# A decoder of two layers in float32r: tile offsets, the first phase and retention's values

## The chip, the core and the metric

One core of one Trainium2 chip runs the whole program in one launch. The time is that of the device from start to end of an execution, in microseconds; beside it stands the span, from the first to the last instruction of one execution that the hardware profiler recorded.

## The reference

256 tokens of width 2048 go through two layers; the first mixes tokens by two kinds of attention, the second by retention. Behind each mixer stand cross-attention to 256 memory rows and a feed-forward part with a convolution over three tokens. All is float32.

```python
def reference(x, mem, positions, ...):
    mem_n = _rmsnorm(mem, norm_mem)
    h = x
    for l in range(DEPTH):
        hn = _rmsnorm(h, norm_mix[l])
        if l % 2 == 0:
            h = h + _mixer_ab(hn, ...)          # block and compressed/selected/window attention
        else:
            h = h + _mixer_c(hn, ...)           # retention
        h = h + _cross_attn(_rmsnorm(h, norm_cross[l]), mem_n, ...)
        h = h + _conv_ffn(_rmsnorm(h, norm_ffn[l]), ...)
    return _rmsnorm(h, norm_final)

def _retention(q, k, v):                        # 8 heads, dk 256, dv 512, chunks of 128
    def step(state, xs):
        qi, ki, vi = xs
        intra = einsum(einsum(qi, ki) * decay, vi)
        cross = einsum(qi, state) * q_dec
        state = state * c_dec + einsum(ki * k_dec, vi)
        return state, intra + cross
```

## The kernel before, in words

Nearly all time goes to products of activations with weights. [...] The weight products use fp32r and split each operand into an upper part (rounded to fp32r) and a lower part (the rest): upper x upper, upper x lower, lower x upper make three products. `weights` (L225) loads 128x1024 pieces of weights by SP's queue, ScalarE writes the upper part (L232), VectorE the lower one (L233).

Two forms of a product exist. `product_b_steps` has weights as the stationary operand and gives outputs with features on the partitions: the upper weights (L272) meet a moving slab of upper and lower tokens side by side, 512 columns, the lower weights (L277) its upper half, 256 columns. `product_a_steps` has tokens stationary and weights moving, 512 columns in most products, 256 and 280 in two early ones (L307 to L309). Each matmul has its own weight load.

Products follow each other without a gap in TensorE's order. Side tasks (attention heads, norms, retention's scores) are generators in a queue, `side`; `pump` (L244) lets the first two of them go a step at each turn of a product, and where a generator yields nothing it places its instructions there. TensorE's order is that of the code; in the first phase (L379 to L414) that of ScalarE and VectorE too; else a scheduler sets it.

The first phase multiplies x with 512 columns of weights before any norm factor is known: `x_in` holds x, `SPANS` (L365) groups its 16 slabs of 128 features in pairs, and each pair is loaded (`load_x`, L371, and L393), split (L197, L200, L401 to L407) and used in two products at once. Their results are added up by `halves` (L326 on ScalarE, L328 on VectorE), which frees the accumulators for the next product (L307). Meanwhile `start_steps` loads the rows of x and squares them on ScalarE (`Norm.add`, L148) for the norm.

In retention a head's scores `pr` (keys x tokens) and values `v` are plain fp32 and meet in three matmuls (L986, L988) that a side task, `attend`, places inside the next product, that of the gate.

Tiles come from a pool in which a tile takes its bytes per partition rounded up to 32. `eps`, one column of 4 bytes, is the first whose 32 bytes are no multiple of 64. As the built program has it, all large tiles that fp32r matmuls read begin 32 bytes behind a multiple of 64. Slabs inside tiles are whole multiples of 64 bytes apart, but for the weights of the 280-column product: three slabs of 1120 bytes stand side by side, so every third (30 of its 96 moving operands) begins on a multiple of 64.

Of the kernel before, what the change touches and what calls it, by code (L numbers as in the profile page):

```python
# [20 lines left out]
P = 128  # L21
# [54 lines left out]
def hybrid_kernel(ctx: ExitStack, tc: tile.TileContext, a, out):  # L76
# [6 lines left out]

    def new(shape, dt=F32, tag=None, bufs=1):
        count[0] += 1
        name = f"t{count[0]}"
        return sb.tile(shape, dt, name=name, tag=tag or name, bufs=bufs)

# [3 lines left out]
    def long():  # L92
        return new([P, 512], F32, "long", 9)
# [15 lines left out]


    ident = new([P, P])
    make_identity(nc, ident)
    ones = new([P, P])
    pool.memset(ones, 1.0)
    eps = new([P, 1])
# [4 lines left out]
    def raw_tile():  # L120
        return new([P, 1024], F32, "raw", 4)
# [242 lines left out]
    held = [[], []]  # L364
    SPANS = [range(k, k + 2) for k in range(0, ND, 2)]  # L365
    ready = [deque(), deque()]
# [3 lines left out]

    def load_x(p):  # L371

        nc.sync.dma_start(x_in[p].rearrange("p s t -> p (s t)"), a["x"][:, 2 * p * S : (2 * p + 2) * S])

# [4 lines left out]
    with tc.manual_schedule(engines=engines):  # L379
        act.activation(new([P, 1]), eps, AF.Copy, scale=eps)  # L380
        load_par(nc.sync, "mix")
        for p in range(ND // 2):
            i, c = p // 2, slice(p % 2 * 512, p % 2 * 512 + 512)
            if p % 2 == 0:
                raws = [raw_tile() for _ in range(2)]
                his = [new([P, 1024], F32R, "whi", 4) for _ in range(2)]
                los = [new([P, 1024], F32R, "wlo", 4) for _ in range(2)]
            if p < 4:
                load_x(p)
            for q in range(2):  # L390
                if p < 4 or p % 2 == 0:
                    d = c if p < 4 else slice(0, 1024)
                    nc.sync.dma_start(raws[q][:, d], w_ab.part(4 * i, 4, 4096 + 256 * q, 256)[:, d])  # L393
            if p == 3:
                for x in range(4, 8):
                    load_x(x)
            for s in (2 * p, 2 * p + 1):
                xs_mix.append(slab_tile())
                xhat_hi(xs_mix[s], x_in[p][:, s % 2, :], gain("mix")[:, s : s + 1])
            if p == 0:  # L400
                dve.tensor_copy(his[0][:, c], raws[0][:, c])  # L401
            for s in (2 * p, 2 * p + 1):
                xhat_lo(xs_mix[s], x_in[p][:, s % 2, :], gain("mix")[:, s : s + 1])
            for q in range(2):
                if p or q:
                    act.activation(his[q][:, c], raws[q][:, c], AF.Copy)
                dve.tensor_sub(los[q][:, c], raws[q][:, c], his[q][:, c].bitcast(F32))  # L407
# [3 lines left out]
            if p == 3:  # L411
# [205 lines left out]
    def mixer_ab(xs, row, col, kcv):  # L617
# [6 lines left out]
        def start_steps():  # L624
            norm = Norm()
            tg = [(t, g) for g in range(4) for t in range(2)]
            for i in range(10):
                if i < 8:
                    load_rows(*tg[i])
                if i > 1:  # L630
                    norm.add(*tg[i - 2])
                if i < 9:
                    yield
            norm.column(col)
            yield
# [6 lines left out]
            yield from angle_steps(0, posi)  # L642
# [19 lines left out]
        def compress(i, kind, t, done):  # L662

            for _ in range(8):
                yield
# [77 lines left out]
        comp = []  # L743
        side.extend((start_steps(), setup_steps()))
        side.append(compress(0, "k", kcv[0], comp))
# [22 lines left out]
        def nsa_group(g, qr, qu):  # L768
# [33 lines left out]
            side.extend(nsa_head(g, r, qr[r]) for r in range(4))  # L802
            yield
            yield
            yield
# [4 lines left out]
            dve.tensor_copy(pct, b[:, 0:S])  # L810
            pcts[g] = pct

        def nsa_head(g, r, q):
            h = 4 * g + r
            p_s = causal(q, ks[0][:, g, :], gate_v[:, :, h, 1])
            p_w = causal(q, ks[1][:, g, :], gate_v[:, :, h, 2])
            yield
            yield
            t_s = causal_t(p_s)
            yield  # L820
            t_w = causal_t(p_w)
            yield
            while len(comp) < 2:
# [104 lines left out]
    def mixer_c(xs, norm, done):  # L928
# [25 lines left out]
        def head(h, os):  # L954
# [16 lines left out]
            def attend():  # L971
# [241 lines left out]
```

## Time and profile before

| | us |
|---|---|
| median of 3 runs | 2832.78 (2832.66 to 2833.45) |
| the profiled execution | 2834.51 |
| its span | 2832.8 |
| TensorE matmul busy | 2812.4 |
| VectorE busy | 1906.3 |
| ScalarE busy | 1460.1 |

A row of a timeline gives start, duration, engine, line and operation, operands, count, and in brackets the idle time before it with what ended it. [...] A group's busy time is that of the union of its records.

### The profile page before, as it was taken

The page shows a single profiled execution, that of the slowest core. Times are in us where ns is not written, and L with a number is a line of the kernel's source. Part 1 is how long each engine was busy: PE and PEld are TensorE (multiplying, and loading weights), DVE is VectorE, ACT ScalarE, POOL GpSimd, SP SyncE. Part 2 cuts the span into 40 slices and gives each one's busy share as a digit, 9 for nine tenths or more (in the row PEclk, how much of TensorE's full clock was granted, in tenths as well). Part 3 has the DMA queues.
Part 4 walks back from the last instruction along what each step waited for, and adds up shares of the span by engine and source line. Part 5 has one row for each costly group of instructions (what it writes and reads, how often), then busy time and mean ns, then how long its engine had stood idle before and what let it go on. Part 6 is the DMA issues. An engine that isn't in the chain of part 4 may idle for free.

```text
span 2832.8 us, 39488 instructions
## 1 busy us (share of the span) xinstructions
PE 2812.4 (99%) x14726; PEld 2406.5 (85%) x14726; DVE 1906.3 (67%) x3147; ACT 1460.1 (52%) x2193; POOL 29.9 (1%) x211
## 2 busy tenths in 40 slices
PE   8999999999999999999999999999999999999998
PEld 7888888888888888888888888888888888888887
DVE  7765776776767677665555555556767767676766
ACT  6454455654545455454444444444665645454544
POOL 0000000000000000000000000000000000000000
PEclk9999999999999999999999999999999999999999
DMA  8535565455555555555555555555545555555554
GB/s 305 171 126 161 180 211 172 170 189 192 187 198 190 189 196 201 194 179 179 179 178 186 193 178 179 182 206 189 189 164 193 186 196 184 193 193 187 197 186 158
DMA packets 150544, 530.11 MB, mean 187 GB/s; under 512 B 17040, under 2 KB 17456, under 8 KB 150352
## 3 DMA queue, kind: packets, MB, share of 16 engines
q1 hardware_dynamic: 148752, 523.65, 54.7%
q0 software_dynamic: 1024, 2.90, 0.3%
q8 instruction: 115, 1.88, 0.3%
q10 hardware_dynamic: 576, 1.05, 0.1%
q14 instruction: 77, 0.63, 0.1%
HBM read 525.43 MB, written 2.10 MB: 186 GB/s over the span
## 4 chain that ended last, share of the span: by engine, by line
PE 98%; DMA 1%; ACT 0%; DVE 0%; SPq 0%; issue 0%; ACTq 0%; DVEq 0%
PE acc L272 32%; PE acc L277 17%; PE acc L307 14%; PE acc L309 14%; PE acc L308 14%; PE bank L350 1%; PE bank L986 0%; DMA t<-in_w_in_ab_dram 0%; PE bank L504 0%; PE bank L496 0%; PE bank L484 0%; DMA t<-in_rows_dram 0%; PE bank L1009 0%; PE bank L589 0%; PE bank L579 0%; PE bank L975 0%
## 5 line engine op out<-in xcount | busy, mean ns | idle before, releaser
L233 DVE TENSOR_TENSOR t<-t,t 128x1024 fp32r<-128x1024 f32 x954 | 1156.6, 1220 | 568.7 <-ACT t L232 522.9
L232 ACT ACTIVATE t<-t 128x1024 fp32r<-128x1024 f32 x954 | 1004.6, 1057 | 739.6 <-PE acc L309 540.6
L272 PE MATMUL acc<-t,t 128*128 128x512 f32 x4096 | 965.9, 391 | 6.2 <-DVE t L200 6.2
L272 PEld LDWEIGHTS acc<-t,t 128*128 128x128 f32 x4096 | 759.7, 188 | 159.1 <-DVE t L200 6.2
L307 PE MATMUL acc<-t,t 128*128 128x512 f32 (+2 forms) x1824 | 713.3, 391 | 4.9 <-DVE t L328 4.9
L309 PE MATMUL acc<-t,t 128*128 128x512 f32 (+2 forms) x1824 | 705.1, 387 | 0.0
L308 PE MATMUL acc<-t,t 128*128 128x512 f32 (+2 forms) x1824 | 704.5, 386 | 0.0
L277 PEld LDWEIGHTS acc<-t,t 128*128 128x128 f32 x4096 | 510.6, 192 | 11.6 <-issue 0.4
L277 PE MATMUL acc<-t,t 128*128 128x256 f32 x4096 | 518.0, 283 | 0.0
L307 PEld LDWEIGHTS acc<-t,t 128*128 128x128 f32 x1824 | 343.9, 189 | 74.7 <-DVE t L328 5.4
L309 PEld LDWEIGHTS acc<-t,t 128*128 128x128 f32 x1824 | 343.6, 188 | 69.5
L308 PEld LDWEIGHTS acc<-t,t 128*128 128x128 f32 x1824 | 343.9, 189 | 68.9 <-issue 1.9
L883 ACT ACTIVATE t<-acc 128x256 f32<-128x256 f32 x176 | 65.8, 374 | 229.6 <-PE acc L272 229.6
L886 DVE TENSOR_TENSOR t<-acc,t 128x256 f32<-128x256 f32 x176 | 74.1, 421 | 157.2 <-ACT t L883 157.2
L889 ACT ACTIVATE t<-t,t 128x256 f32<-128x256 f32 x176 | 103.8, 590 | 1.1
L210 ACT ACTIVATE t<-t 128x256 fp32r<-128x256 f32 x88 | 36.1, 411 | 130.5 <-DVE t L908 130.5
L607 DVE TENSOR_TENSOR t<-t,acc 128x512 f32<-128x512 f32 x148 | 95.1, 680 | 2.8 <-PE acc L1104 2.8
L891 DVE SCALAR_TENSOR_TENSOR t<-t,t,t 128x256 f32<-128x256 f32 x176 | 84.2, 478 | 1.5
L890 DVE SCALAR_TENSOR_TENSOR t<-t,t,t 128x256 f32<-128x256 f32 x176 | 84.2, 478 | 0.2
L326 ACT ACTIVATE t<-acc 128x256 f32<-128x256 f32 x80 | 30.0, 376 | 103.4 <-PE acc L272 103.4
L328 DVE TENSOR_TENSOR t<-acc,t 128x256 f32<-128x256 f32 x80 | 33.4, 419 | 69.7 <-ACT t L326 69.7
L887 DVE TENSOR_TENSOR t<-t,t 128x256 f32<-128x256 f32 x176 | 74.3, 422 | 3.0
(218 smaller groups left out, 1127.6 us busy)
## 6 DMA issues: line engine op xcount, KB each, us to landing
t<-in_w_up_dram SPq DMA_DIRECT2D x352, 512.0 KB, 3.4
t<-in_w_in_c_dram SPq DMA_DIRECT2D x192, 512.0 KB, 3.5
t<-in_w_down_dram SPq DMA_DIRECT2D x176, 512.0 KB, 3.4
t<-in_w_in_ab_dram SPq DMA_DIRECT2D x80, 512.0 KB, 4.2
t<-in_w_out_c_dram SPq DMA_DIRECT2D x64, 512.0 KB, 3.3
t<-in_w_out_ab_dram SPq DMA_DIRECT2D x32, 512.0 KB, 4.2
t<-in_w_kv_x_dram SPq DMA_DIRECT2D x32, 512.0 KB, 3.8
t<-in_w_q_x_dram SPq DMA_DIRECT2D x16, 512.0 KB, 3.2
```

Source lines behind the costliest of these rows:

```text
L232: act.activation(hi[:, 0 : m * ncol], raw[:, 0 : m * ncol], AF.Copy)
L233: dve.tensor_sub(lo[:, 0 : m * ncol], raw[:, 0 : m * ncol], hi[:, 0 : m * ncol].bitcast(F32))
L272: pe.matmul(acc[j], parts[k - k0][0][:, j * P : (j + 1) * P], xs[k], start=(k == 0), stop=(end and k == n - 1))
L277: pe.matmul(acc[j][:, 0:S], parts[k - k0][1][:, j * P : (j + 1) * P], xs[k][:, 0:S], start=False, stop=(end and k == n - 1))
L307: pe.matmul(o, xh, hi, start=(k == 0), stop=False)
L308: pe.matmul(o, xh, lo, start=False, stop=False)
L309: pe.matmul(o, xl, hi, start=False, stop=(k == n - 1))
L607: dve.tensor_add(part(t, g), part(t, g), acc)
L887: dve.tensor_mul(u[:, 2:], t, norm.r)
L889: act.activation(c, u[:, 2:], AF.Identity, bias=cp[:, 3, j : j + 1], scale=cp[:, 2, j : j + 1])
L890: dve.scalar_tensor_tensor(c, u[:, 1 : S + 1], cp[:, 1, j : j + 1], c, op0=ALU.mult, op1=ALU.add)
L891: dve.scalar_tensor_tensor(c, u[:, 0:S], cp[:, 0, j : j + 1], c, op0=ALU.mult, op1=ALU.add)
```

## The change

- Tiles of two dimensions get a second one that is rounded up to a multiple of 64 bytes; the kernel sees the part that it asked for. In the built program all operands of fp32r matmuls then begin on a multiple of 64, but for 30 of the 280-column ones.
- First phase: eight products of a tile of ones with itself stand first in TensorE's order. The first two groups of `SPANS` have one slab, the others two; x stands ahead of the gains in SP's queue, the first weights go by ScalarE's queue, and some pieces use other buffers. The rows of x are loaded a step later and squared four steps later, and the angles of the rotation are a side task of their own.
- Retention: the values are split into upper and lower parts (`vh`, `vl`), the scores too (`ph`, `pl`), and nine fp32r matmuls take the place of three of plain fp32.
- Some side tasks yield more or fewer times.

```diff
     def new(shape, dt=F32, tag=None, bufs=1):
         count[0] += 1
         name = f"t{count[0]}"
+        unit = 64 // mybir.dt.size(dt)
+        if len(shape) == 2 and shape[1] % unit:
+            full = [shape[0], -(-shape[1] // unit) * unit]
+            return sb.tile(full, dt, name=name, tag=tag or name, bufs=bufs)[:, 0 : shape[1]]
         return sb.tile(shape, dt, name=name, tag=tag or name, bufs=bufs)
...
-    SPANS = [range(k, k + 2) for k in range(0, ND, 2)]
+    SPANS = [range(0, 1), range(1, 2)] + [range(k, k + 2) for k in range(2, ND, 2)]
...
-        act.activation(new([P, 1]), eps, AF.Copy, scale=eps)
-        load_par(nc.sync, "mix")
-        for p in range(ND // 2):
-            i, c = p // 2, slice(p % 2 * 512, p % 2 * 512 + 512)
+        warm = bank()
+        for _ in range(8):
+            pe.matmul(warm[:, 0:P], ones, ones, start=True, stop=True)
+        raws = [None, None]
+        for ks in SPANS:
+            p, m = ks[0] // 2, len(ks)
+            c = slice(ks[0] % 4 * 256, ks[0] % 4 * 256 + 256 * m)
...
+            load_x(ks[0], ks[0] + m)
             for q in range(2):
-                if p < 4 or p % 2 == 0:
-                    d = c if p < 4 else slice(0, 1024)
-                    nc.sync.dma_start(raws[q][:, d], w_ab.part(4 * i, 4, 4096 + 256 * q, 256)[:, d])
-            if p == 3:
-                for x in range(4, 8):
-                    load_x(x)
-            for s in (2 * p, 2 * p + 1):
+                (nc.sync if ks[0] else nc.scalar).dma_start(raws[q][:, d], w_ab.part(ks[0] // 4 * 4, 4, 4096 + 256 * q, 256)[:, c])
+            if ks[0] == 0:
+                load_par(nc.sync, "mix")
+                act.activation(new([P, 1]), eps, AF.Copy, scale=eps)
+            for s in ks:
                 xs_mix.append(slab_tile())
...
         def start_steps():
             norm = Norm()
             tg = [(t, g) for g in range(4) for t in range(2)]
-            for i in range(10):
-                if i < 8:
-                    load_rows(*tg[i])
-                if i > 1:
-                    norm.add(*tg[i - 2])
-                if i < 9:
-                    yield
+            for i in range(14):
+                if 0 < i < 9:
+                    load_rows(*tg[i - 1])
+                if i > 5:
+                    norm.add(*tg[i - 6])
+                yield
...
-            v = [long(), long()]
+            vh, vl = [[new([P, 512], F32R, *tag) for _ in range(2)] for tag in (("vh", 2), ("long", 9))]

             def ev_v(t, acc):
-                sm = small(1)
-                act.activation(v[t], acc, AF.Identity, scale=norm.c[:, t : t + 1], accum_out=sm)
+                sm, v = small(1), new([P, 512], F32, "p", 7)
+                act.activation(v, acc, AF.Identity, scale=norm.c[:, t : t + 1], accum_out=sm)
                 dve.tensor_scalar_mul(sm, sm, -1.0 / 512)
-                dve.tensor_scalar_add(v[t], v[t], sm)
+                act.activation(vh[t], v, AF.Identity, bias=sm)
+                dve.scalar_tensor_tensor(vl[t], v, sm, vh[t].bitcast(F32), op0=ALU.add, op1=ALU.subtract)
...
+                ph, pl = new([P, 512], F32R, "p", 7), new([P, 512], F32R, "p", 7)
+                act.activation(ph[:, 0 : S + P], pr[:, 0 : S + P], AF.Copy)
+                dve.tensor_sub(pl[:, 0 : S + P], pr[:, 0 : S + P], ph[:, 0 : S + P].bitcast(F32))
...
-                    pe.matmul(b, pr[:, t * P : (t + 1) * P], v[0], start=True, stop=(t == 0))
-                    if t:
-                        pe.matmul(b, pr[:, S : S + P], v[1], start=False, stop=True)
+                    blocks = [(t * P, 0), (S, 1)][: t + 1]
+                    for c0, i in blocks:
+                        for p_, v_ in ((ph, vh), (ph, vl), (pl, vh)):
+                            pe.matmul(b, p_[:, c0 : c0 + P], v_[i], start=(i == 0 and p_ is ph and v_ is vh),
+                                      stop=(c0 == blocks[-1][0] and p_ is pl))
```

ScalarE's order at the end of the first phase, before: `t_73` and `t_74` are the rows of x, `acc_111` and `acc_112` the sums of the first of the two products, lines L232 write upper parts of the next product's weights.

```order
L406 ACTIVATE t_297<-t_295 128x512
L148 ACTIVATE t_464,t_408<-t_74 128x512
L148 ACTIVATE t_485,t_408<-t_73 128x512
L232 ACTIVATE t_391<-t_390 128x1024
L148 ACTIVATE t_500,t_408<-t_74 128x512
L232 ACTIVATE t_431<-t_430 128x1024
L148 ACTIVATE t_521,t_408<-t_73 128x512
L148 ACTIVATE t_538,t_408<-t_74 128x512
L326 ACTIVATE t_346<-acc_111 128x256
L326 ACTIVATE t_350<-acc_112 128x256
```

The same place after; L417, L237, L153 and L331 are the lines L406, L232, L148 and L326 of before, `acc_117` and `acc_118` the sums of the first product.

```order
L417 ACTIVATE t_307<-t_348 128x512
L237 ACTIVATE t_415<-t_414 128x1024
L153 ACTIVATE t_550,t_432<-t_73 128x512
L331 ACTIVATE t_370<-acc_117 128x256
L237 ACTIVATE t_454<-t_453 128x1024
L331 ACTIVATE t_374<-acc_118 128x256
L153 ACTIVATE t_573,t_432<-t_74 128x512
L153 ACTIVATE t_606,t_432<-t_73 128x512
```

Of the squares that stood ahead of the first evacuation one is left there.

TensorE's order in retention's first head, before: `t_12664` are the scores, `t_12479` and `t_12480` the values, L307 to L309 the gate's product around them.

```order
L309 MATMUL acc_12640<-t_12686,t_12047 128x512
L986 MATMUL bank_12704<-t_12479,t_12664 128x512
L986 MATMUL bank_12709<-t_12479,t_12664 128x512
L988 MATMUL bank_12709<-t_12480,t_12664 128x512
L307 MATMUL acc_12639<-t_12735,t_12053 128x512
```

The same place after: `t_12697` and `t_12698` are the scores' parts, `t_12503` to `t_12506` the values' parts.

```order
L314 MATMUL acc_12670<-t_12720,t_12071 128x512
L1004 MATMUL bank_12738<-t_12503,t_12697 128x512
L1004 MATMUL bank_12738<-t_12505,t_12697 128x512
L1004 MATMUL bank_12738<-t_12503,t_12698 128x512
L1004 MATMUL bank_12745<-t_12503,t_12697 128x512
L1004 MATMUL bank_12745<-t_12505,t_12697 128x512
L1004 MATMUL bank_12745<-t_12503,t_12698 128x512
L1004 MATMUL bank_12745<-t_12504,t_12697 128x512
L1004 MATMUL bank_12745<-t_12506,t_12697 128x512
L1004 MATMUL bank_12745<-t_12504,t_12698 128x512
L312 MATMUL acc_12669<-t_12775,t_12077 128x512
```

Nine fp32r matmuls stand where three of fp32 stood, between the same matmuls of the gate's product.

## Rows read from the trace of the kernel before

**Rows 1.** The page: busy time of each engine, share, instructions

```profile
PE 2812.4 (99%) x14726; PEld 2406.5 (85%) x14726; DVE 1906.3 (67%) x3147; ACT 1460.1 (52%) x2193; POOL 29.9 (1%) x211
```

**Rows 2.** Waits of TensorE: us in total, times, longest

```profile
PE acc L272 <- DVE t L200: 6.2, 1, 6.2
PE acc L307 <- DVE t L328: 4.9, 1, 4.9
```

**Rows 3.** Groups by line and shape: count | busy us, mean ns | idle before

```profile
L272 PE MATMUL acc<-t,t 128*128 128x512 f32 x4096 | 965.9, 391 | 6.2 <-DVE t L200 6.2
L307 PE MATMUL acc<-t,t 128*128 128x512 f32 x1760 | 693.5, 394 | 0.0
...
L277 PE MATMUL acc<-t,t 128*128 128x256 f32 x4096 | 518.0, 283 | 0.0
...
L308 PE MATMUL acc<-t,t 128*128 128x256 f32 x32 | 10.1, 316 | 0.0
```

**Rows 4.** Timeline of TensorE in a feed-forward product, 1000 to 1010 us

```profile
999.73 1.72 PE L277 MATMUL acc<-t,t 128*128 128x256 f32 x13
1001.29 7.44 PE L272 MATMUL acc<-t,t 128*128 128x512 f32 x32
1008.57 1.59 PE L277 MATMUL acc<-t,t 128*128 128x256 f32 x12
```

**Rows 5.** Timeline of TensorE around retention's scores (L975, L977), fp32

```profile
1297.37 1.02 PE L975 MATMUL bank<-t,t 128*128 128x256 f32 x4
1298.23 0.61 PE L977 MATMUL bank<-t,t 128*128 128x128 f32 x4
...
1299.13 0.40 PE L309 MATMUL acc<-t,t 128*128 128x512 f32 x1
1299.37 0.40 PE L307 MATMUL acc<-t,t 128*128 128x512 f32 x1
```

**Rows 6.** Timeline of TensorE, scores x values of one head

```profile
1304.17 1.88 PE L986 MATMUL bank<-t,t 128*128 128x512 f32 x4
...
1306.97 0.40 PE L308 MATMUL acc<-t,t 128*128 128x512 f32 x1
```

**Rows 7.** Timeline of TensorE, starts of three slabs of the 280-column product

```profile
50.38 0.29 PE L307 MATMUL acc<-t,t 128*128 128x280 f32 x1
...
51.16 0.29 PE L307 MATMUL acc<-t,t 128*128 128x280 f32 x1
...
51.93 0.29 PE L307 MATMUL acc<-t,t 128*128 128x280 f32 x1
```

**Rows 8.** Timeline of all engines in the first 11 us

```profile
1.18 0.42 SPq L373 DMA_DIRECT2D t<-in_x_dram  x1
...
4.29 0.91 ACT L197 ACTIVATE t<-t,t 128x256 fp32r<-128x256 f32 x2 [1.97 <-DMA t<-in_x_dram]
...
6.20 2.08 PE L272 MATMUL acc<-t,t 128*128 128x512 f32 x4 [6.20 <-DVE t L200]
...
8.07 1.06 PE L277 MATMUL acc<-t,t 128*128 128x256 f32 x4
...
8.93 1.72 PE L272 MATMUL acc<-t,t 128*128 128x512 f32 x4
...
10.48 1.11 PE L277 MATMUL acc<-t,t 128*128 128x256 f32 x8
```

**Rows 9.** The same timeline at the end of the first phase

```profile
34.17 0.63 ACT L148 ACTIVATE t<-t 128x512 f32<-128x512 f32 x1 [0.25 <-DMA t<-in_rows_dram]
...
34.80 0.64 ACT L326 ACTIVATE t<-acc 128x256 f32<-128x256 f32 x2
...
35.67 0.58 PE L307 MATMUL acc<-t,t 128*128 128x256 f32 x1 [4.94 <-DVE t L328]
```

**Rows 10.** Stretches: us, busy time of each engine, granted clock, DMA share, GB/s

```profile
6.20:30.75 24.55, 24.53 (x128) 21.03 (x128) 17.07 (x39) 16.94 (x36) 3.63 (x9) 1.00 1.00 354
35.67:41.10 5.43, 5.43 (x25) 5.43 (x26) 4.29 (x11) 3.42 (x8) 0.00 (x0) 0.51 0.79 266
800.00:1200.00 400.00, 400.00 (x2126) 346.60 (x2125) 278.08 (x410) 206.11 (x289) 8.10 (x47) 1.00 0.57 194
```

More of the change, by code (lines that the diff above doesn't have):

```diff
@@ L108, in slab_tile @@
         return new([P, 2 * S], F32R, "xs", 32)
+    ones = new([P, P])
+    pool.memset(ones, 1.0)
     ident = new([P, P])
     make_identity(nc, ident)
-    ones = new([P, P])
-    pool.memset(ones, 1.0)
     eps = new([P, 1])
@@ L369, in hybrid_kernel, with load_x @@
     cst, cmask, tri_f, posi = new([P, 4]), new([P, 2, 16]), work((P, P)), new([P, S], I32, "w", 12)
-    def load_x(p):
-        nc.sync.dma_start(x_in[p].rearrange("p s t -> p (s t)"), a["x"][:, 2 * p * S : (2 * p + 2) * S])
+    def load_x(s0, s1):
+        nc.sync.dma_start(x_in[s0 // 2][:, s0 % 2 : s0 % 2 + s1 - s0, :].rearrange("p s t -> p (s t)"),
+                          a["x"][:, s0 * S : s1 * S])
     def load_rows(t, g):
@@ L379, in hybrid_kernel @@
     with tc.manual_schedule(engines=engines):
-        act.activation(new([P, 1]), eps, AF.Copy, scale=eps)
-        load_par(nc.sync, "mix")
-        for p in range(ND // 2):
-            i, c = p // 2, slice(p % 2 * 512, p % 2 * 512 + 512)
-            if p % 2 == 0:
-                raws = [raw_tile() for _ in range(2)]
+        warm = bank()
[5 more added lines that the diff above has]
+            c = slice(ks[0] % 4 * 256, ks[0] % 4 * 256 + 256 * m)
+            if ks[0] % 4 == 0:
                 his = [new([P, 1024], F32R, "whi", 4) for _ in range(2)]
                 los = [new([P, 1024], F32R, "wlo", 4) for _ in range(2)]
-            if p < 4:
-                load_x(p)
-            for q in range(2):
-                if p < 4 or p % 2 == 0:
-                    d = c if p < 4 else slice(0, 1024)
-                    nc.sync.dma_start(raws[q][:, d], w_ab.part(4 * i, 4, 4096 + 256 * q, 256)[:, d])
-            if p == 3:
-                for x in range(4, 8):
-                    load_x(x)
-            for s in (2 * p, 2 * p + 1):
+            if ks[0] in (0, 4, 14):
+                raws = [raw_tile() for _ in range(2)]
+            elif ks[0] in (8, 10, 12):
+                raws = [new([P, 512], F32, "p", 7) for _ in range(2)]
+            d = slice(0, 512) if ks[0] in (8, 10, 12) else c
+            load_x(ks[0], ks[0] + m)
+            for q in range(2):
+                (nc.sync if ks[0] else nc.scalar).dma_start(raws[q][:, d], w_ab.part(ks[0] // 4 * 4, 4, 4096 + 256 * q, 256)[:, c])
[3 more added lines that the diff above has]
+            for s in ks:
                 xs_mix.append(slab_tile())
@@ L400, in hybrid_kernel @@
             if p == 0:
-                dve.tensor_copy(his[0][:, c], raws[0][:, c])
-            for s in (2 * p, 2 * p + 1):
+                dve.tensor_copy(his[0][:, c], raws[0][:, d])
+            for s in ks:
                 xhat_lo(xs_mix[s], x_in[p][:, s % 2, :], gain("mix")[:, s : s + 1])
@@ L405, in hybrid_kernel @@
                 if p or q:
-                    act.activation(his[q][:, c], raws[q][:, c], AF.Copy)
-                dve.tensor_sub(los[q][:, c], raws[q][:, c], his[q][:, c].bitcast(F32))
+                    act.activation(his[q][:, c], raws[q][:, d], AF.Copy)
+                dve.tensor_sub(los[q][:, c], raws[q][:, d], his[q][:, c].bitcast(F32))
                 ready[q].extend((his[q][:, k : k + 256], los[q][:, k : k + 256]) for k in range(c.start, c.stop, 256))
@@ L410, in hybrid_kernel @@
                 next(g, None)
-            if p == 3:
+            if p == 6:
                 for t in (cst, cmask.rearrange("p t n -> p (t n)"), tri_f, posi.bitcast(F32), gain("cross"), gain("conv0")):
@@ L641, in start_steps @@
                     dve.tensor_mul(kcv[i][:, j, :], held[i][j], row)
-            yield from angle_steps(0, posi)
             dve.tensor_copy(cos_k, row)
@@ L662, in compress @@
         def compress(i, kind, t, done):
-            for _ in range(8):
+            for _ in range(2):
                 yield
@@ L743, in mixer_ab @@
         comp = []
-        side.extend((start_steps(), setup_steps()))
+        side.extend((start_steps(), setup_steps(), angle_steps(0, posi)))
         side.append(compress(0, "k", kcv[0], comp))
@@ L802, in nsa_group @@
             side.extend(nsa_head(g, r, qr[r]) for r in range(4))
-            yield
-            yield
-            yield
+            for _ in range(6):
+                yield
             b = bank()
@@ L810, in nsa_group @@
             dve.tensor_copy(pct, b[:, 0:S])
+            yield
+            yield
             pcts[g] = pct
@@ L822, in nsa_head @@
             yield
-            while len(comp) < 2:
+            while len(comp) < 2 or g not in pcts:
                 yield
```

## Prediction

> **What bounds the kernel now.** I read the waits of TensorE first. In 2832.8 us it waits twice for another engine, 6.2 us before its first matmul and 4.9 us in front of the first product with tokens on the partitions [rows 2]; the page gives it as busy for 99% [rows 1]. So outside the first 41 us and the tail the end is set by how closely the matmuls follow each other, and time is won there only by fewer matmuls, cheaper ones, or a smaller spacing. I then looked for that spacing, since the busy times overlap and don't show it. The groups by shape give the counts: 4096 + 3 x 1760 = 9376 fp32r matmuls with 512 moving columns and 4096 + 3 x 32 = 4192 with 256 [rows 3] (the three lines of a product with tokens stationary have the same count, so one of them stands there). The timeline gives the spacing: thirteen matmuls of 256 columns start in 1.56 us, 0.120 us each, and 32 of 512 columns in 7.28 us, 0.2275 us each [rows 4]. [...]
>
> **The rounding to 64 bytes.** It adds no instruction. In the program before, every operand of these matmuls begins 32 bytes behind a multiple of 64, in the program after on one (front part, on the layout). The trace of before holds no full-speed matmul with both operands on a multiple of 64, so the cost has to be bounded. Nearest rows:
> - [...]
> - The product with 280 columns has moving operands at 32 and at 0 by turns. Six matmuls from 0 take 0.78 us, the next six from 32 take 0.77 us [rows 7]: no difference. But 280 columns are 1120 bytes, 17.5 pieces of 64 bytes, and touch 18 pieces from either start. 512 columns touch 32 pieces from a multiple of 64 and 33 from 32 bytes behind one; 256 touch 16 and 17. So these rows exclude a fixed fee for a crooked start, and can't exclude a fee per piece touched. [...]
> - The spacing seems to move in steps of about 7 ns: after a switch from fp32 to fp32r work a single spacing (1299.13 to 1299.37 us) is 0.24 us where the settled ones are 0.2275 us [rows 4, 5].
> [...] I take one piece less per matmul as the value: 13,568 x 6.7 ns = 91 us. [...]
>
> [...]
>
> DVE would not take over: in the feed-forward stretch it is busy 278 of 400 us [rows 10], and the same work in a time 4% shorter is 73%.
>
> **The first phase.** Four terms.
> - Start. x is issued at 1.18 us behind the gains and its first use is at 4.29 us, then two upper parts (0.91 us) and two lower parts stand before the first matmul at 6.20 us [rows 8]. After, x is first in SP's queue, half as large, and the first weights go by ScalarE's queue at the same time; one upper and one lower part (half of 0.91 us each) follow. About 3.9 + 0.5 + 0.5 = 4.9 us: 1.3 us won.
> - Clock. [...] From 6.20 to about 10.2 us half the time, 2.0 us, is lost. [...] Whether the clock is up by then no row shows: bounds 0 and 2.0 us, I take 1.5.
> - The wait of 4.9 us. The evacuation of the first product (L326) stands in ScalarE's queue behind squares of rows (L148), the last of which starts at 34.17 us when its DMA has landed, and so itself starts at 34.80 us; the addition on VectorE follows and TensorE resumes at 35.67 us after 4.94 us of waiting [rows 9], the product having ended at 30.7 us. After, one square stands before the first evacuation and none before the second. That square's 256 KB stand behind 6.3 MB of x and weights and 0.5 MB of weights: at the 354 GB/s of this stretch [rows 10] and a start at 3 us they land near 23 us, before the product ends (about 27.5 us). What is late next is the chain itself: evacuation, a weight part of 1.06 us between the two, evacuation, addition; the first of the two products ends 1.4 us ahead of the second, so some 0.9 us of wait are left. 4.0 us won.
> - The second slow stretch. Granted clock 0.51 from 35.67 to 41.10 us, after TensorE had stood since 30.7 us [rows 10]: half of 5.4 us, 2.7 us, go with the wait.
> Against them 0.5 us for the small first pieces (each waits for its own DMA). Sum 9.0 us, bounds 4 and 11. The later squares give the row factors later; the products of the mixer hide that as before (no wait of TensorE there in rows 2), and a wait would have no cover, since TensorE's order is fixed.
>
> **Retention.** The three fp32 matmuls of a head with the values stand as six records between 1304.17 and 1306.97 us, where one ordinary spacing belongs to the next product: 2.80 - 0.23 = 2.57 us [rows 6]. After there are nine fp32r matmuls, 9 x 0.2275 = 2.05 us, or 9 x 0.221 = 1.99 us in the first case, and the change back to fp32r work falls away (two spacings of 0.24 us). Eight heads: 8 x 0.58 = 4.7 us. The added upper and lower parts (two more ScalarE copies per head and a third for the scores, subtractions instead of an addition on VectorE) lie beside the gate's product of the same head, 96 x 0.2275 = 21.8 us of matmuls; both engines have room [rows 10]. If that cover were gone, the matmuls behind them in TensorE's order would wait 1 to 2 us a head, 8 to 16 us.
>
> **The sum.** The profiled execution took 2834.5 us with a span of 2832.8 us; the runs have a median of 2832.8 us. Differences of the span are applied to that median: 2832.8 - 91 - 9.0 - 4.7 = 2728 us.
>
> **The rivals.**
> 1. *One piece less per matmul*: 2728 us, its own range 2716 to 2740. [...] Against: nothing shows that a read goes by 64 bytes. Chance 0.40.
> 2. [...] Chance 0.24.
> 3. *The rounding does nothing*, the excess belongs to fp32r: 2832.8 - 13.7 = 2819 us, 2815 to 2827 with the bounds of the first phase. For it: the 280-column rows as they stand. The change would then not do what its first part says. Chance 0.30.
> 4. *Slower*: weight loads and moving reads that begin at the same offset collide, and the settled spacing becomes the 0.24 us of after a switch: 2832.8 + 91 - 13.7 = 2910 us. The rest of the change covers 13.7 us, so it decides from 1 ns per matmul on. Against it: both operands had a common offset (32) before as well. Chance 0.06.
>
> **How the numbers follow.** The predicted time is the first case's, 2728 us. The range 2674 to 2824 us holds the first case, most of the third and more than half of the second, about 0.83 in all. A measurement here can't tell 0.2% (5.7 us) from no change. Faster by more: cases 1 and 2 and most of 3, 0.89; within: the rest of 3, 0.05; slower: case 4, 0.06.
>
> **What would show it.** The start-to-start spacing of 512 and 256 columns away from the ends: 0.220 and 0.113 us for case 1, 0.216 and 0.110 for case 2, unchanged for case 3, 0.233 or more for case 4. First matmul of the first product at about 4.9 us, first tokens product at about 28.5 us with no granted clock of 0.5 before it. The retention block about 2.0 us from its first matmul to the next product's. I am wrong if the spacing is unchanged and the time fell by much more than 14 us, or if TensorE shows new waits in the mixer.

## The result, and the profile after

The change makes the kernel slower: 2849.56 us median (2848.92 to 2850.60, 6 runs) beside 2832.77 us (2832.39 to 2834.89, 6 runs) of before, a ratio of 1.0058 with a 95% interval of 1.0045 to 1.0071. The forecast was 2728 us, the range ended at 2824 us. The profiled execution took 2849.58 us with a span of 2847.8 us, 15.0 us more than the span before.

The page and the groups by shape, against [rows 1, 3]. TensorE is busy for longer, and the groups say with which matmuls: those with weights moving (L312, which was L307) have 5.8 us more and the two lines behind it (L313 and L314, which were L308 and L309) 9.3 and 8.7 us more, those with 512 slab columns (L277, was L272) 5.7 us more, those with 256 (L282, was L277) 13.8 us less. The page after:

```profile
PE 2833.2 (99%) x14766; PEld 2394.7 (84%) x14766; DVE 1913.9 (67%) x3158; ACT 1475.5 (52%) x2218; POOL 30.1 (1%) x211
```

The two groups of before that [rows 3] leaves out, and the groups after:

```profile
L309 PE MATMUL acc<-t,t 128*128 128x512 f32 x1760 | 685.7, 390 | 0.0
L308 PE MATMUL acc<-t,t 128*128 128x512 f32 x1760 | 685.0, 389 | 0.0
```

```profile
L277 PE MATMUL acc<-t,t 128*128 128x512 f32 x4096 | 971.6, 393 | 2.2 <-DVE t L205 2.2
L312 PE MATMUL acc<-t,t 128*128 128x512 f32 x1760 | 699.3, 397 | 0.0
L314 PE MATMUL acc<-t,t 128*128 128x512 f32 x1760 | 694.4, 395 | 0.0
L313 PE MATMUL acc<-t,t 128*128 128x512 f32 x1760 | 694.3, 395 | 0.0
L282 PE MATMUL acc<-t,t 128*128 128x256 f32 x4096 | 504.2, 279 | 0.1
```

The waits of TensorE, against [rows 2]: two of 11.1 us together have become five of 5.2 us. So the waits fell by 6 us while the time grew by 15: the loss stands between matmuls that wait for no engine.

```profile
PE acc L277 <- DVE t L205: 2.2, 2, 1.5
PE bank L495 <- DVE t L487: 1.1, 1, 1.1
PE bank L388 <- POOL t L117: 1.0, 1, 1.0
PE acc L312 <- DVE t L333: 0.9, 1, 0.9
```

The timeline of TensorE after, against [rows 4 and 6]: 32 matmuls of 512 columns with slabs moving start in 7.33 us (0.229 each; it was 0.2275), 32 of 256 columns in 3.77 us (0.118; it was 0.120). A spacing is read from start to start, since the records overlap: those of L277 last 393 ns in the mean. With weights moving, 20 spacings lie between the rows at 1301.19 and 1305.85, in 4.66 us: 0.233 each. Retention's nine (L1004) take 2.09 us to the next product's first.

```profile
999.22 7.49 PE L277 MATMUL acc<-t,t 128*128 128x512 f32 x32
1006.55 3.93 PE L282 MATMUL acc<-t,t 128*128 128x256 f32 x32
1010.32 2.00 PE L277 MATMUL acc<-t,t 128*128 128x512 f32 x8
...
1301.19 0.40 PE L312 MATMUL acc<-t,t 128*128 128x512 f32 x1
...
1305.85 0.40 PE L314 MATMUL acc<-t,t 128*128 128x512 f32 x1
1306.09 2.25 PE L1004 MATMUL bank<-t,t 128*128 128x512 f32 x9
1308.18 0.39 PE L312 MATMUL acc<-t,t 128*128 128x512 f32 x1
```

The start of the first phase and its end, against [rows 8, 9]: the first product begins at 5.09 us, its 256-column matmuls are 0.12 us apart from the first on (5.67 to 5.91 us), it stands 1.54 us ahead of its third group, and the next product begins at 30.16 us and stands once more, 0.86 us, three matmuls later.

```profile
1.00 3.41 PE L388 MATMUL bank<-t 128*128 128x128 f32 x16 [1.00 <-POOL t L117]
5.09 0.74 PE L277 MATMUL acc<-t,t 128*128 128x512 f32 x2 [0.68 <-DVE t L205]
5.67 0.40 PE L282 MATMUL acc<-t,t 128*128 128x256 f32 x2
5.91 0.63 PE L277 MATMUL acc<-t,t 128*128 128x512 f32 x2
...
9.99 1.19 PE L277 MATMUL acc<-t,t 128*128 128x512 f32 x4 [1.54 <-DVE t L205]
...
30.16 0.38 PE L312 MATMUL acc<-t,t 128*128 128x256 f32 x1
...
31.63 0.38 PE L312 MATMUL acc<-t,t 128*128 128x256 f32 x1 [0.86 <-DVE t L333]
```

The stretches, against [rows 10] (length, busy time of PE, PEld, DVE, ACT, POOL, granted clock, DMA share, GB/s): the 0.51 of the granted clock after the first phase is gone.

```profile
5.09:30.16 25.07, 23.30 (x128) 19.52 (x128) 18.36 (x46) 17.84 (x37) 3.57 (x9) 1.00 1.01 365
31.63:36.10 4.47, 4.47 (x39) 4.47 (x40) 4.26 (x11) 4.47 (x12) 0.00 (x0) 1.00 1.04 396
```

Where the change can reach the spacing is the address of tiles. In the built program of before, weight parts and slabs both begin 288 bytes behind a multiple of 512. After, the weight parts stand at 320 and the slabs at 384: the dummy tile of ScalarE's first activation, made ahead of the loop before, is now made inside it, between the weight parts and the slabs, and with the rounding it takes 64 bytes. I call the slab's address less the weight part's, modulo 256, the *distance*: 0 before, 64 after. Theory D says that the distance sets the spacing (theory 1 in the expectations below); theory O, its rival, that the offset of each operand from a multiple of 64 does (theory 2). With slabs moving, the moving operand's address less the stationary one's is the distance; with weights moving it is the negative of it.

### The profile page after: what moved, and what is told of

It is laid out like the page before. It is cut to its first block, busy times and chain, and to the rows that moved or that the text cites. A ratio compares the mean times of both kernels' runs of the same rounds, so it can differ in the third digit from the quotient of the medians.

```text
span 2847.8 us, 39615 instructions
## 1 busy us (share of the span) xinstructions
PE 2833.2 (99%) x14766; PEld 2394.7 (84%) x14766; DVE 1913.9 (67%) x3158; ACT 1475.5 (52%) x2218; POOL 30.1 (1%) x211
## 3 DMA queue, kind: packets, MB, share of 16 engines
q0 software_dynamic: 1024, 2.90, 0.3%
## 4 chain that ended last, share of the span: by engine, by line
PE 98%; DVE 0%; DMA 0%; issue 0%; ACT 0%; SPq 0%; POOL 0%; DVEq 0%
PE acc L277 32%; PE acc L282 16%; PE acc L312 15%; PE acc L313 15%; PE acc L314 15%; PE bank L355 1%; PE bank L1004 1%; PE bank L515 0%; PE bank L507 0%; PE bank L495 0%; PE bank L1026 0%; PE bank L600 0%; PE bank L987 0%; PE bank L590 0%; DMA t<-in_x_dram 0%; PE bank L505 0%
## 5 line engine op out<-in xcount | busy, mean ns | idle before, releaser
L237 ACT ACTIVATE t<-t 128x1024 fp32r<-128x1024 f32 x954 | 1006.0, 1057 | 748.3 <-PE acc L314 537.9
L277 PE MATMUL acc<-t,t 128*128 128x512 f32 x4096 | 971.6, 393 | 2.2 <-DVE t L205 2.2
L277 PEld LDWEIGHTS acc<-t,t 128*128 128x128 f32 x4096 | 757.8, 188 | 160.7 <-ACT t L417 2.0
L312 PE MATMUL acc<-t,t 128*128 128x512 f32 (+2 forms) x1824 | 717.7, 393 | 1.0 <-DVE t L333 0.9
L314 PE MATMUL acc<-t,t 128*128 128x512 f32 (+2 forms) x1824 | 712.5, 391 | 0.0
L313 PE MATMUL acc<-t,t 128*128 128x512 f32 (+2 forms) x1824 | 712.5, 391 | 0.0
L282 PEld LDWEIGHTS acc<-t,t 128*128 128x128 f32 x4096 | 496.5, 188 | 12.8 <-DVE t L238 0.6
L282 PE MATMUL acc<-t,t 128*128 128x256 f32 x4096 | 504.2, 279 | 0.1
L314 PEld LDWEIGHTS acc<-t,t 128*128 128x128 f32 x1824 | 341.8, 187 | 80.7
L312 PEld LDWEIGHTS acc<-t,t 128*128 128x128 f32 x1824 | 341.9, 187 | 80.3 <-DVE t L333 1.4
L313 PEld LDWEIGHTS acc<-t,t 128*128 128x128 f32 x1824 | 342.0, 188 | 78.5
L331 ACT ACTIVATE t<-acc 128x256 f32<-128x256 f32 x80 | 30.0, 377 | 99.6 <-PE acc L277 97.0
```

The costliest lines, as they stand in the source:

```text
L237: act.activation(hi[:, 0 : m * ncol], raw[:, 0 : m * ncol], AF.Copy)
L277: pe.matmul(acc[j], parts[k - k0][0][:, j * P : (j + 1) * P], xs[k], start=(k == 0), stop=(end and k == n - 1))
L282: pe.matmul(acc[j][:, 0:S], parts[k - k0][1][:, j * P : (j + 1) * P], xs[k][:, 0:S], start=False, stop=(end and k == n - 1))
L312: pe.matmul(o, xh, hi, start=(k == 0), stop=False)
L313: pe.matmul(o, xh, lo, start=False, stop=False)
L314: pe.matmul(o, xl, hi, start=False, stop=(k == n - 1))
```

## The experiments

**Streams of equal matmuls.** A program without the model; each stream has one stationary and one moving operand at chosen offsets:

```diff
+COUNT = 64
...
+st, mv = w[:, s // 4 : s // 4 + P], m[:, o // 4 : o // 4 + n]
+for k in range(COUNT):
+    pe.matmul(accs[i % 2][:, 0:n], st, mv, start=(k == 0), stop=(k == COUNT - 1))
```

> This kernel leaves the model out. It runs streams of 64 fp32r matmuls with one fixed stationary and one fixed moving operand each, 512 or 256 columns, between short fp32 matmuls; the offsets of the two operands modulo 512 bytes are set per stream. Theory 1, the spacing depends on the distance between the two operands: streams with both at 0, 4, 16 or 32 bytes have one spacing, 0.227 us for 512 and 0.120 us for 256 columns; streams with a distance of 64 or 448 bytes have another, 0.229 to 0.234 and 0.113 to 0.118 us, whatever the absolute offset. Theory 2, it depends on the absolute offset in 64 bytes: both at 32 gives 0.227 and 0.120 us, every stream with both on a multiple of 64 gives 0.229 to 0.234 and 0.113 to 0.118 us, distance 0 too. Theory 3, neither: all streams of one length agree within 2 ns.

Mean spacing in ns over the last 32 of a stream, from the starts in the trace, by moving less stationary address:

| bytes | 0 | 16 | 32 | 64 | 96 | 128 | 192 | 256 | 320 | 384 | 448 |
|---|---|---|---|---|---|---|---|---|---|---|---|
| 512 columns | 226.7 | 231.7 | 233.3 | 228.8 | 233.4 | 233.3 | 233.3 | 226.7 | 228.9 | 232.6 | 233.3 |
| 256 columns | 120.0 | 116.7 | 116.7 | 117.8 | 119.9 | 118.5 | 113.3 | 120.0 | 117.8 | 118.5 | 113.3 |

It repeats after 256 bytes, within 0.7 ns; 512 and 1024 give the values of 0. With both operands 32 bytes off a multiple of 64 it is 226.7 and 120.0 too, and with both on one it takes all the values of the columns 0, 64, 128 and 192, so O falls. D holds only for operands on a multiple of 32: with both 16 or 4 bytes off, 512 columns take 230.0 and 237.7 ns at distance 0, where D expected 227. One stream more departs from D: with the stationary operand at 32 and the moving one at 480, which is the distance 192, 256 columns take 117.8 and not 113.3 ns. In the table's streams at 0, 64 and 192 the two lengths add up to 346.6 ns: what 512 columns lose, 256 win. A product with slabs moving has as many of one as of the other and hardly feels the distance 64 (916.4 + 480.9 us before, 922.3 + 467.2 us with the tile of 64 below); a product with weights moving has 512 columns alone. Four streams of 64 in the trace, in the first two the operands stand 512 bytes apart (distance 0), in the others 960 (distance 192):

```profile
360.94 14.78 PE L58 MATMUL acc<-m,w 128*128 128x512 f32 x64
...
375.92 7.92 PE L58 MATMUL acc<-m,w 128*128 128x256 f32 x64
...
430.25 15.18 PE L58 MATMUL acc<-m,w 128*128 128x512 f32 x64
...
445.62 7.51 PE L58 MATMUL acc<-m,w 128*128 128x256 f32 x64
```

**The rounding alone.** Before, with the lines of `new` that round; the distance stays 0.

```diff
+unit = 64 // mybir.dt.size(dt)
+if len(shape) == 2 and shape[1] % unit:
+    full = [shape[0], -(-shape[1] // unit) * unit]
+    return sb.tile(full, dt, ...)[:, 0 : shape[1]]
```

> The kernel before with the rounding to 64 bytes alone; slabs and weight parts stay a multiple of 512 bytes apart, and both begin on a multiple of 64. Theory 1 (distance): spacing 0.227 and 0.120 us as before, 2833 us (2830 to 2836). Theory 2 (absolute offset): the slower spacing of after without the gains of the first phase and retention, about 2863 us.

2832.66 us, ratio 0.9999 [0.9989, 1.0009]: nothing.

**The tile alone.** Before, not rounded, with an unused tile of 64 bytes where the dummy stands after. Three sizes of it were run later, to see whether D gives numbers.

```diff
+if p == 0:
+    pool.memset(new([P, 16]), 0.0)     # 64 bytes; [P, 32], [P, 48], [P, 64] for 128, 192, 256
```

> The kernel before, not rounded, with one unused tile of 64 bytes between the weight parts and the slabs of activations, so that their distance becomes 64 (or 448) modulo 512 while both still begin 32 bytes behind a multiple of 64. Theory 1 (distance): product with tokens stationary 0.233 us per 512 columns (5280 x 6 ns = 32 us more), the other 0.229 us per 512 (4096 x 1.5 ns = 6 us more) and 0.117 us per 256 columns (4096 x 3.4 ns = 14 us less), 2857 us (2850 to 2864). Theory 2 (absolute offset): 2833 us.

> Before, with an unused tile of 128 bytes between weight parts and slabs. If each pair's distance modulo 256 sets the spacing as in the streams: 5,226 matmuls of 512 columns with the weights moving at 232.6 ns in place of 226.7 (+31 us), 4,005 with the slabs moving at 233.3 (+27 us), 3,998 of 256 columns at 118.5 in place of 120.0 (-6 us): 2885 us. If any distance other than 0 costs the same as 64 bytes did: 2858 us.

> Before, with an unused tile of 192 bytes in that place. By the streams: weights moving 228.9 ns (+11.5 us), slabs moving 512 columns at 233.3 (+27 us), 256 columns at 113.3 (-27 us): 2844 us; with the 117.8 ns of the second set of streams 2862 us. If any distance other than 0 costs the same as 64 bytes did: 2858 us.

> Before, with an unused tile of 256 bytes in that place. If the distance counts modulo 256, as in the streams: 2833 us, the spacing of before. If it counts modulo 512 or more, or a tile moved anywhere costs: 2845 us or more.

Sums of the spacings of each kind (us) and medians. Counted are the spacings from the mixer's first product on where the next matmul is fp32r too: 5,216, 4,011 and 3,997 of the three kinds in before and the programs made from it, 5,226, 4,005 and 3,998 in after and those made from it. "Lower shift" is told below:

| kernel | distance | 512, weights moving | 512, slabs | 256, slabs | median | ratio to before |
|---|---|---|---|---|---|---|
| before | 0 | 1192.6 | 916.4 | 480.9 | 2832.8 | |
| rounding alone | 0 | 1192.5 | 916.3 | 480.8 | 2832.7 | 0.9999 [0.9989, 1.0009] |
| tile of 64 | 64 | 1225.1 | 922.3 | 467.2 | 2857.8 | 1.0088 [1.0073, 1.0103] |
| tile of 128 | 128 | 1220.8 | 936.2 | 476.5 | 2877.0 | 1.0155 [1.0141, 1.0169] |
| tile of 192 | 192 | 1203.0 | 938.2 | 457.1 | 2841.5 | 1.0029 [1.0018, 1.0040] |
| tile of 256 | 0 | 1192.6 | 916.4 | 480.9 | 2832.3 | 0.9998 [0.9988, 1.0007] |
| after | 64 | 1224.1 | 921.5 | 467.2 | 2849.6 | 1.0058 [1.0045, 1.0071] |
| after, dummy early | 0 | 1191.5 | 915.5 | 481.0 | 2825.2 | 0.9972 [0.9961, 0.9983] |
| lower shift | mixed | 1216.7 | 915.8 | 472.7 | 2841.8 | 1.0031 [1.0020, 1.0043] |

By D 2857, 2885, 2844 and 2833 us were expected, and 2857.8, 2877.0, 2841.5 and 2832.3 measured. An unused tile of 64 bytes costs 25 us, one of 128 costs 44, one of 192 costs 8.5, one of 256 nothing. At 128 the forecast from the streams is 8 us too high: the slabs' 512 columns lose 20 us where 27 were expected. The rows of the tile of 64 (0.113 us per 256 columns, 0.229 per 512) and of the tile of 128 (16 of 512 columns in 3.73 us, 0.233 each) follow. After's rows above, at the same distance 64, have 0.118 us per 256 columns: stretches of 32 show the one value or the other in both programs (113 ns in 42 of 110 with the tile of 64, in 41 of 112 after), so a single stretch can mislead, and the sums agree (467.2 us in both). Which of the two a stretch takes isn't shown.

```profile
1000.75 3.79 PE L277 MATMUL acc<-t,t 128*128 128x256 f32 x32
1004.38 7.49 PE L272 MATMUL acc<-t,t 128*128 128x512 f32 x32
1011.70 0.52 PE L277 MATMUL acc<-t,t 128*128 128x256 f32 x3
```

```profile
1500.08 3.89 PE L272 MATMUL acc<-t,t 128*128 128x512 f32 x16
1503.81 0.39 PE L307 MATMUL acc<-t,t 128*128 128x512 f32 x1
```

**After, with the dummy tile made early.**

```diff
     ident_bf = new([P, P], BF16)
+    dummy = new([P, 1])
...
-                act.activation(new([P, 1]), eps, AF.Copy, scale=eps)
+                act.activation(dummy, eps, AF.Copy, scale=eps)
```

> The kernel after with the tile of the first ScalarE instruction made ahead of all others, so that it no longer lies between the weight parts and the slabs; rounding, first phase and retention stay. Theory 1 (distance): spacing back to 0.227 and 0.120 us, 2819 us (2814 to 2825). Theory 2 (absolute offset): 2849 us as after.

2825.17 us, ratio 0.9972 [0.9961, 0.9983]: faster than before, by about 8 us and not by the 13.7 forecast for the first phase and retention. The spacing of before is back, 18 of 512 columns in 4.08 us (0.227 each) and 32 of 256 in 3.83 us (0.120), and the span is 24.7 us shorter than after's (2823.1 against 2847.8). In the table the three sums of after fall by 32.6 and 6.0 us and rise by 13.8: 24.8 us, so the spacings are all of it.

```profile
998.77 4.24 PE L278 MATMUL acc<-t,t 128*128 128x512 f32 x18
1002.85 4.00 PE L283 MATMUL acc<-t,t 128*128 128x256 f32 x32
1006.68 5.63 PE L278 MATMUL acc<-t,t 128*128 128x512 f32 x24
```

**First phase and retention apart.** One kernel is the last with retention as before, the other is before with retention's diff alone.

```diff
-            vh, vl = [[new([P, 512], F32R, *tag) for _ in range(2)] for tag in (("vh", 2), ("long", 9))]
+            v = [long(), long()]
...
-                        for p_, v_ in ((ph, vh), (ph, vl), (pl, vh)):
+                    pe.matmul(b, pr[:, t * P : (t + 1) * P], v[0], start=True, stop=(t == 0))
```

> The kernel after with the dummy tile made early (distance 0) and retention as before: the first phase, the rows squared later, and the rounding, which the run before this has shown to cost nothing. If the first phase gives what I predicted (9.0 us): 2823.8 us, and retention is then worth some 1.4 us less than nothing beside the 2825.2 us measured with it. If retention gives its 4.7 us: 2829.9 us, and the first phase gives only 3 us. If the new wait of 1.3 us in the attention takes a part: 2825 us.

> Before, with retention's values and weights in upper and lower parts and nothing else; the distance between weight parts and slabs stays 0. By my prediction 4.7 us less than before: 2828.1 us. If the nine matmuls per head at their measured 0.231 us each replace the six passes of fp32 less exactly: 2831 to 2833 us, no change that can be measured. If the added ScalarE and VectorE work is waited for: above 2834 us.

Without retention's part: 2828.88 us, 0.9986 [0.9977, 0.9995], span 2827.1. Retention alone: 2828.81 us, 0.9985 [0.9976, 0.9994], span 2828.7, 4.1 us less than before's. The timed gains are 4.2 and 4.3 us, each known to about 2.5 us; the spans give 5.7 and 4.1. The first kernel's rows show what its part won and lost. The first product begins at 4.93 us, the next at 30.25 us after 1.02 us of waiting, and this stands a second time, 0.84 us, three matmuls later; the first product of the mixer begins at 55.69 us. In the timeline of before (last row below) that one begins at 62.39 us, after the same matmuls but for the eight constant ones, so 6.7 us are won by then; the span ends with 5.7.

```profile
4.93 1.22 PE L278 MATMUL acc<-t,t 128*128 128x512 f32 x2
5.95 0.62 PE L283 MATMUL acc<-t,t 128*128 128x256 f32 x2
6.37 0.66 PE L278 MATMUL acc<-t,t 128*128 128x512 f32 x2
...
30.25 0.39 PE L313 MATMUL acc<-t,t 128*128 128x256 f32 x1 [1.02 <-DVE t L334]
...
31.71 0.39 PE L313 MATMUL acc<-t,t 128*128 128x256 f32 x1 [0.84 <-DVE t L334]
...
55.69 1.64 PE L278 MATMUL acc<-t,t 128*128 128x512 f32 x6
```

```profile
62.39 1.32 PE L272 MATMUL acc<-t,t 128*128 128x512 f32 x5
```

These 6.7 us are measured against one execution. The wait ahead of the second product, 4.9 us in the trace of before, is 3.2 to 5.0 us in the programs that have its first phase: 3.2 with the tiles of 128 and 256, 3.5 with the rounding, 4.4 with the tiles of 64 and 192, 5.0 with retention alone (below the row with the rounding). The profiled execution of before is also 1.7 us longer than its median, that of the first kernel stands at its median; this accounts for the difference between 5.7 and 4.2.

```profile
PE acc L311 <- DVE t L332: 3.5, 1, 3.5
```

**The attention's yields.** After with the dummy early shows two sets of transposes (L496) back to back at 221 us, the second waiting 1.04 us for VectorE. The yields of before, with the rest as after:

```diff
-            for _ in range(6):
+            for _ in range(3):
                 yield
...
             dve.tensor_copy(pct, b[:, 0:S])
-            yield
-            yield
...
-            while len(comp) < 2 or g not in pcts:
+            while len(comp) < 2:
```

> The kernel after with the dummy tile made early (distance 0) and the attention's yields as before (three yields ahead of a group's transposes, none behind them, no wait for the group's selection), the first phase, the rows squared later and retention as after. If those yields make the new wait of 1.0 us behind L488: 2824 us, and the gap of 1.3 us between two transposes at 221 us is gone. If it comes from the later start of the rows' squares: 2825 us with the gap still there.

2823.73 us, 0.9967 [0.9955, 0.9979]: the wait is gone, the span 1.2 us shorter (2821.9). This version is the fastest that was run, 9.3 us below the 2833.0 us of before beside it. The transposes with the yields of after, and then with those of before:

```profile
220.99 0.49 PE L496 MATMUL bank<-t,t 128*128 128x128 f32 x3
222.52 0.61 PE L496 MATMUL bank<-t,t 128*128 128x128 f32 x3 [1.04 <-DVE t L488]
```

```profile
222.89 0.49 PE L496 MATMUL bank<-t,t 128*128 128x128 f32 x3
223.13 1.17 PE L278 MATMUL acc<-t,t 128*128 128x512 f32 x4
```

**A try for more: only the lower weight parts shifted.** If each pair's own distance counted, the upper parts could stay at 0, where 512 columns are cheapest, and the lower ones go to 192, where 256 columns are.

```diff
                 his = [new([P, 1024], F32R, "whi", 4) for _ in range(2)]
+                if ks[0] == 0:
+                    pool.memset(new([P, 16]), 0.0)
                 los = [new([P, 1024], F32R, "wlo", 4) for _ in range(2)]
+                if ks[0] == 0:
+                    pool.memset(new([P, 48]), 0.0)
```

> The kernel after with the dummy tile made early, and 64 bytes between the upper and the lower weight parts and 192 bytes behind the lower ones: the upper parts stay at distance 0 from the slabs (modulo 256), the lower parts come to 192 where slabs move over them (256 columns) and to 64 where they move themselves (512 columns). If the spacing goes by each pair's own distance as in the streams: 4,096 matmuls of 256 columns at 113.3 ns in place of 120.0 (-27.3 us) and 1,824 of 512 columns at 228.8 in place of 226.7 (+3.8 us), so 2825.2 - 23.5 = 2802 us. If what the 256 columns save is given back by the 512 columns of the same slab (the sum of the two spacings was the same at distances 0, 64 and 192): 2829 us.

2841.82 us, 1.0031 [1.0020, 1.0043]: a miss for both expectations. The 256 columns won 8 us of 27, and the weights' product lost 25 us where 4 were expected (last row of the table, against that of after with the dummy early). There upper and lower weights move in turn, and all three matmuls rose from 227 to 231 to 232 ns, those at distance 0 too. So a pair's spacing hangs also on its neighbours in the stream. The 256 columns stand 32 in a row at the distance 192 and take 0.118 us each (3.77 us below), where the tile of 192 had 113 ns in 103 of 110 such stretches: this is again the second value, and the neighbours in the row don't explain it. D thus gives the time where all pairs of a product have one distance, and even there 256 columns have two values.

```profile
1004.19 3.93 PE L283 MATMUL acc<-t,t 128*128 128x256 f32 x32
1007.96 4.27 PE L278 MATMUL acc<-t,t 128*128 128x512 f32 x18
```

**More streams, for the mechanism.** Distances between those above, then 64 and 32 stationary columns, then two stationary operands in turn.

```diff
+s = st[k % len(st)] // 4
+pe.matmul(accs[i % 2][0:q, 0:n], w[:, s : s + q], mv, start=(k == 0), stop=(k == COUNT - 1))
```

> Leaves the model out: streams of 48 fp32r matmuls, first with one stationary operand and one moving operand at more distances, then with 64 and 32 stationary columns in place of 128, then with two stationary operands in turn. [...] With two stationary operands in turn, at distances 0 and 192 or 0 and -64: the mean of both spacings either way (230.0 ns at 512 columns, 116.7 ns at 256); if the moving operand meets the load of the NEXT stationary operand, the matmul at distance 0 shows the long spacing (233.3) and the other the short one (226.7); if it meets its own, the reverse. At the new distances no 512-column stream is expected below 226.7 ns and no 256-column stream below 113.3 ns.

Nothing fell below 226.7 and 113.3 ns. With 64 stationary columns 512 moving ones took 228.3 to 231.2 ns, with 32 of them 230.9 to 233.3; at distance 0 this is 229.7 and 231.7 ns, more than the 226.7 with 128. The weight load itself fell from 188 to 134 and 108 ns in the same trace, so the spacing doesn't follow it. Two stationary operands in turn at distances 0 and -64 gave 228.5 and 231.5 ns for 512 columns, mean 230.0, as expected for the mean; 226.7 and 233.3 were expected for the two, whichever load a moving operand meets, its own or the next, so the spread fits neither. And 256 columns at 192 settled at 117.8 ns with one stationary operand here, at 113.3 with two of them 256 bytes apart, and at 113.3 in the table above. What inside TensorE or SBUF makes the spacing depend on the distance is open.

## Why the prediction was wrong, point by point

1. *Spacing sets the end.* Right, and stronger than I used it: the waits fell by 6 us and the time rose, since 5,226 matmuls took 5.6 ns more. (The share of VectorE in a time 4% shorter would have been 72%, not 73%; nothing hangs on it.)
2. *The rounding, -91 us.* This is the step that failed. It says "I take one piece less per matmul as the value", on the premise that what counts is each operand's offset from a multiple of 64. No run shows that a piece of 64 bytes less saves 6.7 ns, so the 91 us of the sum and of the fourth rival were my estimate; nor is a step of 7 ns shown, for in the trace of after, from 100 us on, 226, 229, 231, 233 and 236 ns each stand over 800 times between two starts. Measured: 0 us for the rounding alone. In the streams both operands 32 bytes off and both on a multiple of 64 give the same 226.7 and 120.0 ns. In its place the runs show a price that my sum put at nothing: the tile that moved in between set the operands 64 bytes apart, and that alone costs 25 us. The distance between the two operands counts, and no term of my sum had it: I compared offsets before and after and never the two operands with each other. The fourth rival came nearest. It had the sign and, for the weights' products, the spacing of 0.233 us, but the condition the wrong way round: operands "that begin at the same offset collide", where the same offset is the best case for 512 columns. Its own counterargument, that both had a common offset before as well, should have led to the question whether they still have one. They don't, by the moved line `act.activation(new([P, 1]), ...)`, which the diff shows and which I took for a matter of ScalarE's order. Without that move the change takes 2825.2 us, inside the third rival's 2815 to 2827.
   The rows of the 280-column product couldn't have warned me: their slabs of 1120 bytes stand 96 bytes apart modulo 256, so the rows that I read for the offsets held the distances 96 and 192 as well, and their 0.78 and 0.77 us for six [rows 7] are the same. Over all 96 spacings of that trace the means at the distances 0, 96 and 192 are 130.0, 129.5 and 128.4 ns: what 512 and 256 columns show hardly shows at 280.
3. *The other rivals.* The third had the rounding right: 2832.7 against 2832.8 us. A common offset isn't free everywhere, though: with both operands 16 bytes off a multiple of 64, 512 columns took 230.0 ns, and 4 bytes off 237.7. What the second case rests on is shown by no run: its signs were 0.216 and 0.110 us, and the lowest fp32r streams are at 226.7 and 113.3 ns.
4. *The first phase, -9.0 us.* Measured -6.7 us up to the mixer against one execution of before, of which the attention's new wait gave 1.0 back; 4.2 us by the timed runs. Start: 1.27 us, as forecast. First product, -1.5 for the clock and +0.5 for small pieces: -0.2 us together in the kernel without retention's part, since it still had some 0.8 us of slow spacing (0.21 us per 256 columns at 5.95 us) and stands 0.9 us for its small pieces; after itself has 0.34 us for its first spacing, then 0.24 us per 512 columns and 0.12 per 256, but waits 1.54 us at 9.99. The 1.5 was my estimate, which no run shows by itself, and that the clock was behind the slow start isn't shown either: the granted clock reads 1.00 from 6.20 to 10.48 us of before. The twelve matmuls there take 4.28 us and would take 2.29 at the settled spacings (8 x 0.2267 + 4 x 0.120), so 2.0 us are lost, as the prediction has it. The wait ahead of the next product: from 4.94 us to 1.02, 3.9 us won of 4.0; but 4.94 is one execution's wait, and with the 3.2 to 5.0 us that it has elsewhere the timed runs needn't show all of it. The second slow stretch, 2.7: 1.3 us, which is what the 6.7 leave for it, for the granted clock stays at 1.00 (30.25 to 36.00 us of the kernel without retention's part) but a second wait of 0.84 us, for the second half of the sums, has taken the place of a part of it. That wait is the term that I left out. Two figures of mine don't follow from my own terms: the first product would end near 28.4 us and not at 27.5, so that the next begins near 29.3 (30.25 was measured, and 28.5 named as the sign), and bounds of 4 and 11 us give the third rival 2817 to 2824 us.
5. *Retention, -4.7 us.* Right: 4.1 us by the span, 4.3 timed [-6.8, -1.7, from the ratio]. My sum used 1.99 us for a block, from the first case; without that case I had 2.05, and 2.09 was measured after (eight times 0.58 is also 4.6 and not 4.7).
6. *No wait in the mixer.* Wrong, by 1.0 us at L495, made by the yields and not by the later squares.

The sum with measured terms: 2832.8 + 23.9 (span with the tile of 64) - 6.7 + 1.0 - 4.1 = 2846.9 us, against a span of 2847.8; what the 0.9 us are stays open.

## What to carry to other kernels

A change that makes, rounds or moves a tile can move the tiles behind it: compare the addresses of the operands that meet in the hot matmuls, before and after, modulo 256 and against each other. Fix that layout on purpose, by making small tiles first, since 64 unused bytes cost here three times what the work on the first phase and retention won. When nobody can name what sets a spacing, bound the forecast by both signs and try offsets in a stream of equal matmuls before trusting a rule for it.

## What the runs showed of the hardware

- fp32r matmuls with 128 stationary columns, in stream programs with a mean granted clock of 0.998, start every 226.7 ns (512 columns) and 120.0 ns (256) when both operands begin on a multiple of 32 bytes and their addresses differ by a multiple of 256, and every 228.8 to 234.8 and 113.3 to 120.0 ns at the other distances tried. No 512-column stream was faster; most streams of 256 columns were, down to 113.3 ns.
- With the stationary operand at 0, the first set of streams keeps the sum of the two lengths at 346.6 ns at the distances 0, 64 and 192: what one length loses there, the other wins. With the stationary operand at 32 the distance 192 gives 351.1 ns.
- 256 columns have two values at one distance: 113.3 and 117.8 ns at 192 in the streams, and 113 or 118 ns by stretches of 32 at 64 in the kernels.
- 280 columns hardly feel the distance: 130.0, 129.5 and 128.4 ns at 0, 96 and 192 in the trace of before.
- Neighbours count: with moving operands that alternate between the distances 0 and 64, all matmuls of the weights' product rose from 227 to 231 to 232 ns, those at distance 0 too.
